# Entering a seven-product up projection by halves of the tokens, with four pairs' first products computed ahead

## The chip, the core and the metric

The kernel runs on one core of a Trainium2 chip as a single launch. The metric is the device time of that core in microseconds (us), and less is better. The engines and their names in the profile: TensorE (PE, and PEld for its weight loads), VectorE (DVE), ScalarE (ACT), GpSimd (POOL) and SyncE (SP), which issues the DMAs; "SPq" is its queue.

## The reference

The program is one layer of a first block (a retention and pooling mixer, cross attention, a convolutional gated feed-forward network) followed by two layers of a second block. The change is at the seam of cross attention and the feed-forward network. Cut to what matters there:

```python
x = x + cross_attn(...)                 # its last step is o @ wo
h = rmsnorm(x, ffn_norm_g)              # x * rsqrt(mean(x*x) + eps) * g
a = h @ w_up                            # 1024 tokens x 1024 features -> 2 x 22 x 128
c = conv_w[0]*a2 + conv_w[1]*a1 + conv_w[2]*a + conv_b   # a1, a2: a shifted by 1, 2 tokens
gate, val = jnp.split(c, 2, axis=-1)
x = x + (jax.nn.silu(gate) * val) @ w_down
```

## The kernel before

Activations stand transposed: `xT[0..7]` are eight tiles of 128 features by 1024 tokens. Every fp32 operand is split into a high part (a cast on ACT) and a low part (a subtraction on DVE), and a product is three matmuls per 128 features: high by high, low by high, high by low. One product of a 128x512 result over 512 features is 12 matmuls.

**The projection `xa_wo`** (L793-798) makes x after cross attention, in eight blocks `ft` of 128 output features by two halves of 512 tokens. For each block and half, `residual_add` (L653) adds the result to `xT`, squares it on ACT and sums the squares into `acc` on POOL, and the half is stored to DRAM. Blocks 0 to 5 run both halves in turn, blocks 6 and 7 run the first half of both and then the second.

**The norm** (`norm_half`, L882) then takes one token half at a time: four transposes of `acc` on PE (L889), a sum on DVE (L890), a reciprocal square root by ten small DVE instructions (L304-309), a broadcast by four small matmuls (L894), a copy to `rb` (L895), and eight multiplications of `xT` by `rb` and the gain (L897).

**The up projection** takes its 44 output blocks as 22 pairs of a gate and a value block and computes a pair with seven products instead of eight. The normalised input is seen as a 2x2 block matrix: B11 and B21 are features 0-511 and 512-1023 of the first token half, B12 and B22 the same of the second. The products use B11, B21, B22 and four sums of them, T1 to T4 (`token_blocks`, L903). T1, T3, B22 and T4 share storage with `ahi_t`/`alo_t`, the input of the projection before. Products 1 and 2 read only B11 and B21; the other five read T1 to T4 or B22. Of the weights, four units per pair are split into `whi`/`wlo` (three buffers each): unit 0 is the raw gate weights (products 1 and 2), unit 1 `sm` (products 5 and 6), unit 2 product 7, unit 3 products 3 and 4. The sums of weights are made on POOL (L838-840, L866). Products accumulate in PSUM; ACT copies the running sum out after a product ("P1", "U2", "W", L939-941), and DVE adds such a copy to another product to get a result half (L952, L975, L984). Each result goes through the convolution (ACT L929, DVE L930 and L931), the gate through silu (L967), the two are multiplied (L977) and stored to `hid_d` (L978).

**The down projection** (L1032) reads `hid_d` back (`hidden`, L1009), splits it, and accumulates over groups of 6, 8 and 8 hidden blocks; `x` is re-loaded from DRAM for its residuals (L1033, L655).

What sets the order: up to the second block a scheduler orders every engine's instructions by its own cost estimates, and each engine then runs its list in order. Only from the second block on (L1101) is PE held to written order.

The result of one half in one step, and a product:

```python
mm(ps, whi[:, k], hi[:, k], ...)   # L878
mm(ps, whi[:, k], lo[:, k], ...)   # L879
mm(ps, wlo[:, k], hi[:, k], ...)   # L880
```

## Time and profile before

| what | value |
|---|---|
| time, median of 3 runs | 2691.21 us (2689.56 to 2697.92) |
| the profiled execution | 2690.13 us, of which the span is 2688.3 us |
| PE busy | 2577.1 us, 96% of the span |
| DVE, ACT, POOL busy | 1747.6, 1113.5, 518.0 us |

The three runs differ by 8 us; the profiled execution lies 1.1 us under their median. Times inside the trace count from the start of the span. "PEclk" is the granted TensorE clock as a share of full speed. A bracket such as [5.21 <-DVE hr L309] says that the engine was idle for 5.21 us before this instruction, and what released it.

### The profile page before, as it was taken

What the parts mean: (1) busy time and instruction counts of PE and PEld (TensorE: products, weight loads), DVE (VectorE), ACT (ScalarE), POOL (GpSimd) and SP (SyncE); (2) the same over time, 40 slices, a digit from 0 to 9 for tenths busy, and PEclk for the clock granted to TensorE, in tenths of its full rate; (3) what the DMA queues carried; (4) which work ended last, traced back from release to release, by engine and by line L of the source; (5) the groups of instructions that cost most, each with busy time, mean ns of one, the idle gap of its engine ahead of it and who ended that gap; (6) DMA issues with size and microseconds to landing.
All of it is one profiled execution on the core that took longest, in us unless ns stands there. A gap on an engine that the chain in (4) does not pass through costs nothing. (4 is left out here: it accounts for less than half of the span.)

```text
span 2688.3 us, 36856 instructions
## 1 busy us (share of the span) xinstructions
PE 2577.1 (96%) x13750; PEld 2162.3 (80%) x13750; DVE 1747.6 (65%) x3501; ACT 1113.5 (41%) x2279; POOL 518.0 (19%) x426
## 2 busy tenths in 40 slices
PE   7999999998699999999999999999988999999998
PEld 7888888886588878778778888878876788888898
DVE  8544735434677777842458798575776887777755
ACT  6221334432454444521227774344545443434432
POOL 4112021013333434100121010000143211121101
PEclk9999999998799999999999999999998999999999
DMA  7211141221122222451224443776533222221331
GB/s 252 95 40 37 58 145 44 60 85 55 39 71 88 77 75 90 167 201 47 79 72 126 118 137 105 213 251 199 171 109 114 93 77 81 87 82 64 106 114 71
DMA packets 174118, 282.17 MB, mean 105 GB/s; under 512 B 35522, under 2 KB 103652, under 8 KB 173684
## 3 DMA queue, kind: packets, MB, share of 16 engines
q1 hardware_dynamic: 173940, 279.82, 32.0%
q8 instruction: 108, 1.77, 0.3%
q14 instruction: 70, 0.57, 0.1%
HBM read 206.78 MB, written 72.99 MB: 104 GB/s over the span
## 5 line engine op out<-in xcount | busy, mean ns | idle before, releaser
L1090 PE MATMUL g<-ahi_t,whi 128*128 128x512 f32 x1120 | 466.6, 417 | 3.7 <-DVE y L1624 3.7
L1092 PE MATMUL g<-ahi_t,wlo 128*128 128x512 f32 x1120 | 443.2, 396 | 0.0
L1091 PE MATMUL g<-alo_t,whi 128*128 128x512 f32 x1120 | 441.3, 394 | 0.0
L239 ACT CAST whi<-wraw 128x1024 fp32r<-128x1024 f32 (+1 forms) x172 | 178.6, 1038 | 516.3 <-PE g L272 389.8
L272 PE MATMUL g<-alo_t,whi 128*128 128x512 f32 x832 | 324.1, 391 | 0.6 <-DVE alo_t L293 0.6
L271 PE MATMUL g<-ahi_t,whi 128*128 128x512 f32 x832 | 323.6, 391 | 0.0
L240 DVE TENSOR_TENSOR wlo<-wraw,whi 128x1024 fp32r<-128x1024 f32 (+1 forms) x172 | 212.5, 1237 | 106.1 <-ACT whi L239 105.2
L275 PE MATMUL g<-ahi_t,wlo 128*128 128x512 f32 x832 | 263.1, 390 | 0.0
L1092 PEld LDWEIGHTS g<-ahi_t,wlo 128*128 128x128 f32 x1120 | 212.5, 190 | 47.7
L1090 PEld LDWEIGHTS g<-ahi_t,whi 128*128 128x128 f32 x1120 | 213.4, 190 | 43.7 <-issue 4.4
L1091 PEld LDWEIGHTS g<-alo_t,whi 128*128 128x128 f32 x1120 | 213.5, 191 | 36.7
L655 DVE TENSOR_TENSOR xT<-g,xT 128x512 f32<-128x512 f32 x80 | 51.9, 687 | 234.9 <-PE g L275 218.8
L271 PEld LDWEIGHTS g<-ahi_t,whi 128*128 128x128 f32 x832 | 156.2, 188 | 32.7 <-DVE xT L655 0.5
L272 PEld LDWEIGHTS g<-alo_t,whi 128*128 128x128 f32 x832 | 156.1, 188 | 32.5 <-DVE alo_t L293 0.9
L275 PEld LDWEIGHTS g<-ahi_t,wlo 128*128 128x128 f32 x832 | 156.0, 188 | 32.2
L930 DVE SCALAR_TENSOR_TENSOR c<-a,par,c 128x1024 f32<-128x1024 f32 x44 | 84.8, 1926 | 102.4 <-ACT c L929 102.4
L642 POOL TENSOR_TENSOR acc<-acc,sq 128x512 f32<-128x512 f32 x42 | 73.2, 1762 | 372.9 <-ACT sq L640 372.9
L238 POOL TENSOR_TENSOR wraw<-wraw,par 128x1024 f32<-128x1024 f32 x32 | 65.5, 2048 | 220.1 <-DMA wraw<-in_w_blocks_dram 69.7
L292 ACT CAST pth<-m 128x512 fp32r<-128x512 f32 (+2 forms) x112 | 48.4, 433 | 98.6 <-PE m L1886 81.1
L838 POOL TENSOR_TENSOR sm<-rv 128x512 f32<-128x512 f32 x22 | 29.5, 1342 | 282.8 <-DMA rv<-in_w_blocks_dram 282.8
L271 PE MATMUL g<-hh,whi 128*128 128x512 f32 x192 | 75.0, 401 | 8.4 <-DVE xT L655 8.4
L878 PE MATMUL m<-ahi_t,whi 128*128 128x512 f32 x176 | 69.5, 396 | 8.7 <-ACT ahi_t L292 8.5
(594 smaller groups left out, 6072.7 us busy)
## 6 DMA issues: line engine op xcount, KB each, us to landing
wraw<-in_w_blocks_dram SPq DMA_DIRECT2D x164, 512.0 KB
rv<-in_w_blocks_dram SPq DMA_DIRECT2D x22, 512.0 KB
rg<-in_w_blocks_dram SPq DMA_DIRECT2D x22, 512.0 KB
hid_d<-c SPq DMA_DIRECT2D x22, 512.0 KB
hraw<-hid_d SPq DMA_DIRECT2D x22, 512.0 KB
x_d<-xT SPq DMA_DIRECT2D x32, 256.0 KB
kq_d<-kq SPq DMA_DIRECT2D x16, 512.0 KB
kq<-kq_d SPq DMA_DIRECT2D x16, 512.0 KB
```

Of the source, the lines that this page charges most:

```text
L238: nc.gpsimd.tensor_tensor(raw, raw, prm(gain, 0, nk).unsqueeze(2).to_broadcast(list(raw.shape)), op=ALU.mult)
L239: nc.scalar.copy(hi, raw)
L240: nc.vector.tensor_sub(lo, raw, hi.bitcast(F32))
L271: mm(ps[hf], whi[:, kt, :], hi[kt][:, c], start=(kt == order[0]), stop=False)
L272: mm(ps[hf], whi[:, kt, :], lo[kt][:, c], start=False, stop=False)
L275: mm(ps[hf], wlo[:, kt, :], hi[kt][:, c], start=False, stop=(kt == order[-1]))
L642: nc.gpsimd.tensor_tensor(acc[:, c], acc[:, c], sq, op=ALU.add)
L878: mm(ps, whi[:, k], hi[:, k], start=(start and k == 0), stop=False, **more)
L930: v.scalar_tensor_tensor(out=c, in0=a[:, 1:1 + S], scalar=par[:, 1, 44 + j:45 + j], in1=c, op0=ALU.mult, op1=ALU.add)
L1090: mm(po, whi[:, i, cs], ahi[kt][:, c], start=(i == 0), stop=False)
L1091: mm(po, whi[:, i, cs], alo[kt][:, c], start=False, stop=False)
L1092: mm(po, wlo[:, i, cs], ahi[kt][:, c], start=False, stop=(i == len(kts) - 1))
```

## The change

The norm's work is cut into `norm_stat`, a generator whose first step makes the transposes and the reciprocal square root and whose second makes the broadcast. PE is held to written order from the projection `xa_wo` on. There, blocks 0 to 3 run both halves in turn; then blocks 4 to 7 run the first half, the first token half's transposes stand, and blocks 4 to 7 run the second half (their weights are loaded and split twice). The broadcast for the first half stands two blocks later, still inside the projection.

For the first half the multiplications and the splits of B11 and B21 are made as before. For the second half, ACT multiplies features 0-511 by the gain and DVE forms B22 minus B12 from values that are not yet normalised (L924, L925). Then products 1 and 2 of the first four pairs (`AHEAD`) are computed, copied and added into a buffer `two` of 128x2x512 and stored to a DRAM array `up_d` (L935). `two` is a name with a single buffer, which holds in turn the broadcast of the first half, the four pairs' results, and `both`, into which products 1 of pairs 0 and 1 are loaded back. The second half's transposes stand behind pair 0's products, its broadcast behind pair 1's. After that the second half is normalised and T2, T3, T1, B22 and T4 are formed by other sums of the same blocks: T3 from the difference made earlier, T2 by one addition, T4 on POOL as before (L955).

Pairs 0 and 1 then go through their five remaining products side by side, pairs 2 and 3 one at a time; a re-loaded result is added by DVE where an ACT copy stood. Pairs 4 to 21 keep all seven products in the order 1, 2, 6, 3 of the pair before, 5, 4 of the pair before, 7. There are four buffers `a` for conv inputs instead of three, and the load-ahead of down weights is by three and stands at the end of the pairs instead of by two behind the first six hidden blocks. Core of the diff:

```diff
+AHEAD = 4
-        for ft in range(6):
+        mano.enter_context(tc.manual_schedule(engines={mybir.EngineType.PE}))
+        for ft in range(4):
             gemm_ft(lambda hf, ps: xo_put(ft, hf, ps))
-        w67 = [wtake(), wtake(1)]
-        for hf in range(2):
-            for ft in (6, 7):
-                half_ft(w67[ft - 6], hf, lambda hf, ps: xo_put(ft, hf, ps))
+        for ft in range(4, 8):
+            half_ft(wtake(), 0, lambda hf, ps: xo_put(ft, hf, ps))
+        stat = norm_stat(acc, 0)
+        for ft in range(4, 8):
+            half_ft(wtake(), 1, lambda hf, ps: xo_put(ft, hf, ps))
+            if ft < 6:
+                rps = next(stat)
...
+    def two():
+        return stp.tile([128, 2, 512], F32, tag="two", name="two")
...
-    norm_half(0)
+    rb = two()[:, 0]
+    nc.scalar.copy(rb, rps)
+    for k in range(8):
+        v.scalar_tensor_tensor(out=xT[k][:, h0], in0=xT[k][:, h0], scalar=prm("ffn_norm_g", k), in1=rb, op0=ALU.mult, op1=ALU.mult)
+        put("B11" if k < 4 else "B21", k % 4, xT[k][:, h0])
+    for k in range(4):
+        nc.scalar.activation(out=xT[k][:, h1], in_=xT[k][:, h1], func=AF.Copy, scale=prm("ffn_norm_g", k))
+        v.scalar_tensor_tensor(out=xT[k][:, h1], in0=xT[k + 4][:, h1], scalar=prm("ffn_norm_g", k + 4), in1=xT[k][:, h1],
+                               op0=ALU.mult, op1=ALU.subtract)
     up_make(3)
-    norm_half(1)
-    token_blocks()
+    stat = norm_stat(acc, 1)
+    for j in range(AHEAD):
+        X, y, st = pg(), pg(), two()
+        product(X, 1, j, True)
+        nc.scalar.copy(st[:, 0], X)
+        product(y, 2, j, True)
+        v.tensor_tensor(st[:, 1], y, st[:, 0], op=ALU.add)
+        nc.sync.dma_start(out=up_d[j], in_=st)
+        up_make()
+        if j < 2:
+            rps = next(stat)
+    rb = acc[:, h0]
+    nc.scalar.copy(rb, rps)
+    for k in range(4):
+        v.tensor_tensor(xT[k][:, h1], xT[k][:, h1], rb, op=ALU.mult)
+        v.tensor_tensor(xT[k][:, h0], xT[k][:, h1], xT[k][:, h0], op=ALU.add)
+        put("T2", k, xT[k][:, h0])
+    for k in range(4):
+        put("T3", k, xT[k][:, h1])
+    for k in range(4):
+        b22 = xT[k + 4][:, h1]
+        v.scalar_tensor_tensor(out=b22, in0=b22, scalar=prm("ffn_norm_g", k + 4), in1=rb, op0=ALU.mult, op1=ALU.mult)
+        t1 = res.tile([128, 512], F32, tag="sq", name="t1", bufs=2)
+        v.tensor_tensor(t1, b22, xT[k][:, h0], op=ALU.subtract)
+        put("T1", k, t1)
+    for k in range(4):
+        put("B22", k, xT[k + 4][:, h1])
+        nc.gpsimd.tensor_tensor(xT[k + 4][:, h0], xT[k + 4][:, h0], xT[k][:, h0], op=ALU.subtract)
+    for k in range(4):
+        put("T4", k, xT[k + 4][:, h0])
...
+    both = two()
+    for j in range(2):
+        nc.sync.dma_start(out=both[:, j], in_=up_d[j, :, 0])
+    for j in range(2):
+        p6(j, both[:, j])
+    for j in range(2):
+        p7(j)
+        up_make()
+    for j in range(2):
+        p5(j)
+        c22(j)
+        up_make()
+    for j in range(2):
+        p3(j)
+    for j in range(2):
+        p4_(j)
+        up_make()
+    for j in range(2, NFF + 1):
+        if AHEAD <= j < NFF:
+            p12(j)
+            up_make()
...
+    wahead(wnext[0] + 3)
-    wahead(wnext[0] + 2)
```

How the instructions stand on PE before, from the last matmuls of `xa_wo` on: behind them come the transposes (L889), the broadcast (L894) and the first pair's products.

```order
L284 MATMUL g<-ahi_t,whi 128x512
L285 MATMUL g<-alo_t,whi 128x512
L286 MATMUL g<-ahi_t,wlo 128x512
L889 MATMUL m<-cst,acc 128x128 x4
L894 MATMUL m<-cst,hr 128x128 x4
L889 MATMUL m<-cst,acc 128x128 x4
L878 MATMUL g<-B11h,whi 128x512
L878 MATMUL g<-B21h,whi 128x512
L879 MATMUL g<-B11l,whi 128x512
L880 MATMUL g<-B11h,wlo 128x512
```

And now, on PE, the transposes of the first token half, behind the last of the first-half matmuls; the `g` matmuls below them are second halves of the projection.

```order
L288 MATMUL g<-ahi_t,whi 128x512
L289 MATMUL g<-alo_t,whi 128x512
L290 MATMUL g<-ahi_t,wlo 128x512
L664 MATMUL m<-cst,acc 128x128 x4
L288 MATMUL g<-ahi_t,whi 128x512
L289 MATMUL g<-alo_t,whi 128x512
L290 MATMUL g<-ahi_t,wlo 128x512
```

And the transposes of the second token half, between the products 2 of pair 0 and 1 of pair 1.

```order
L910 MATMUL g<-B21h,whi 128x512
L911 MATMUL g<-B21l,whi 128x512
L912 MATMUL g<-B21h,wlo 128x512
L664 MATMUL m<-cst,acc 128x128 x4
L910 MATMUL g<-B11h,whi 128x512
L911 MATMUL g<-B11l,whi 128x512
```

The small matmuls of the norm have moved from the end of the projection into it, and between products that read only the first token half.

On ACT before, the last casts for T1 to T4 and the copies of the first sums out of PSUM (`xT4` to `xT7` into `ahi_t` are T4, `xT2` and `xT3` into it T1 and into `T2h` T2, `t3` is T3):

```order
L292 CAST ahi_t_81<-t3_5120 128x512
L292 CAST ahi_t_81<-xT5_2709 128x512
L292 CAST ahi_t_81<-t3_5135 128x512
L292 CAST ahi_t_81<-xT2_2706 128x512
L292 CAST ahi_t_81<-xT3_2707 128x512
L292 CAST T2h_4980<-xT2_2706 128x512
L292 CAST whi_5246<-rg_5034 128x512
L292 CAST whi_5246<-rv_5035 128x512
L292 CAST T2h_4980<-xT3_2707 128x512
L292 CAST ahi_t_81<-xT6_2710 128x512
L292 CAST ahi_t_81<-xT7_2711 128x512
L941 COPY P1_5167<-g_5154 128x512
```

On ACT now, the same place (`xT4` to `xT7` into `ahi_t` are T4, `t1` is T1, `two_5237` is the buffer of pair 3's stored results):

```order
L296 CAST ahi_t_81<-xT4_2709 128x512
L296 CAST T2h_5033<-xT2_2707 128x512
L296 CAST ahi_t_81<-xT5_2710 128x512
L296 CAST T2h_5033<-xT3_2708 128x512
L296 CAST whi_5265<-rrv_5178 128x512
L296 CAST ahi_t_81<-xT6_2711 128x512
L296 CAST ahi_t_81<-xT7_2712 128x512
L932 COPY two_5237<-g_5235 128x512
L296 CAST ahi_t_81<-t1_5295 128x512
L296 CAST ahi_t_81<-t1_5300 128x512
L296 CAST ahi_t_81<-t1_5305 128x512
L296 CAST ahi_t_81<-t1_5310 128x512
```

Pair 3's copy now stands behind all four T4 casts and ahead of the T1 casts, and a cast of T2 behind the first of T4.

On DVE before, the end of the sums (the last two `alo_t` rows are T4, `a` is a conv input):

```order
L293 TENSOR_TENSOR T2l_4981<-xT2_2706,T2h_4980 128x512
L293 TENSOR_TENSOR wlo_5247<-rg_5034,whi_5246 128x512
L293 TENSOR_TENSOR wlo_5247<-rv_5035,whi_5246 128x512
L293 TENSOR_TENSOR T2l_4981<-xT3_2707,T2h_4980 128x512
L293 TENSOR_TENSOR alo_t_82<-xT6_2710,ahi_t_81 128x512
L293 TENSOR_TENSOR alo_t_82<-xT7_2711,ahi_t_81 128x512
L952 TENSOR_TENSOR a_5182<-g_5169,P1_5167 128x512
L952 TENSOR_TENSOR a_5280<-g_5267,P1_5265 128x512
L293 TENSOR_TENSOR wlo_5284<-rv_5186,whi_5283 128x512
L984 TENSOR_TENSOR a_5243<-m_5230,W_5228 128x512
```

On DVE now, from the last T4 low part on (`two_5237` as above, `two_5338` is `both`, `wlo_5383` is product 7's weights of pair 1):

```order
L297 TENSOR_TENSOR alo_t_82<-xT7_2712,ahi_t_81 128x512
L934 TENSOR_TENSOR two_5237<-g_5236,two_5237 128x512
L297 TENSOR_TENSOR alo_t_82<-t1_5295,ahi_t_81 128x512
L297 TENSOR_TENSOR alo_t_82<-t1_5300,ahi_t_81 128x512
L951 TENSOR_TENSOR t1_5305<-xT6_2711,xT2_2707 128x512
L951 TENSOR_TENSOR t1_5310<-xT7_2712,xT3_2708 128x512
L297 TENSOR_TENSOR alo_t_82<-t1_5305,ahi_t_81 128x512
L297 TENSOR_TENSOR alo_t_82<-t1_5310,ahi_t_81 128x512
L1017 TENSOR_TENSOR two_5338<-g_5341,two_5338 128x512
L297 TENSOR_TENSOR wlo_5383<-rrv_5226,whi_5382 128x512
L1017 TENSOR_TENSOR two_5338<-g_5355,two_5338 128x512
```

The two additions to `both`, and the weight split behind the first of them, stand behind pair 3's addition and the T1 low parts.

## Rows read from the trace of the kernel before

**Rows 1.** The page, part 1: busy time and share of each engine over the whole span.

```profile
PE 2577.1 (96%) x13750; PEld 2162.3 (80%) x13750; DVE 1747.6 (65%) x3501; ACT 1113.5 (41%) x2279; POOL 518.0 (19%) x426
```

**Rows 2.** Windows: entry, the 22 pairs, start of the down projection.

```profile
core 0: us, PE busy (x) PEld busy (x) DVE busy (x) ACT busy (x) POOL busy (x), PEclk, DMA share, GB/s
648.00:714.00 66.00, 34.91 (x111) 24.71 (x110) 49.06 (x88) 23.75 (x39) 22.82 (x14) 0.66 0.06 20
714.00:1122.00 408.00, 406.29 (x1765) 330.41 (x1764) 299.11 (x275) 201.01 (x257) 143.41 (x118) 1.00 0.24 83
1134.00:1160.00 26.00, 17.64 (x69) 13.88 (x69) 14.71 (x17) 8.96 (x10) 0.00 (x0) 0.87 0.96 353
```

**Rows 3.** Timeline of TensorE, 639 to 715: start, duration, work, [idle before <-releaser].

```profile
639.80 0.39 PE L284 MATMUL g<-ahi_t,whi 128*128 128x512 f32 x1
...
648.42 0.39 PE L286 MATMUL g<-ahi_t,wlo 128*128 128x512 f32 x1
648.65 0.60 PE L889 MATMUL m<-cst,acc 128*128 128x128 f32 x4
654.46 2.04 PE L894 MATMUL m<-cst,hr 128*128 128x128 f32 x8 [5.21 <-DVE hr L309]
...
706.65 0.80 PE L878 MATMUL g<-T2h,whi 128*128 128x512 f32 x1 [7.08 <-ACT P L941]
...
710.65 0.51 PE L878 MATMUL g<-T2h,whi 128*128 128x512 f32 x1
...
714.27 0.39 PE L878 MATMUL g<-ahi_t,whi 128*128 128x512 f32 x1
```

**Rows 4.** Timeline of VectorE, the same stretch.

```profile
654.15 0.16 DVE L309 SCALAR_TENSOR_TENSOR hr<-rs_a,hr 128x4 f32<-128x4 f32 x1
657.16 5.39 DVE L897 SCALAR_TENSOR_TENSOR xT<-xT,par,rb 128x512 f32<-128x512 f32 x8 [2.85 <-ACT rb L895]
...
663.07 2.49 DVE L293 TENSOR_TENSOR B11l<-xT,B11h 128x512 fp32r<-128x512 f32 x4
```

**Rows 5.** Timeline of GpSimd, the same stretch.

```profile
650.61 1.71 POOL L642 TENSOR_TENSOR acc<-acc,sq 128x512 f32<-128x512 f32 x1
...
688.25 6.49 POOL L912 TENSOR_TENSOR xT<-xT,xT 128x512 f32<-128x512 f32 x2 [12.36 <-DVE xT L911]
...
706.74 1.28 POOL L838 TENSOR_TENSOR sm<-rv 128x512 f32<-128x512 f32 x1 [1.18 <-DMA rv<-in_w_blocks_dram]
```

**Rows 6.** Timeline of SyncE's queue (SPq): a weight load.

```profile
702.54 0.33 SPq L835 DMA_DIRECT2D rv<-in_w_blocks_dram  x1
```

**Rows 7.** SyncE's queue in a later stage: store of x, next load into its buffer.

```profile
1732.18 1.83 SPq L1571 DMA_DIRECT2D x_d<-x  x2
...
1735.64 0.92 SPq L1569 DMA_DIRECT2D x<-x_d  x2
```

**Rows 8.** VectorE, the instruction that takes this load.

```profile
1739.85 0.75 DVE L1570 SCALAR_TENSOR_TENSOR x<-x,par,rfb 128x512 f32<-128x512 f32 x1 [3.45 <-DMA x<-x_d]
```

**Rows 9.** Groups of instructions by line, 714 to 1122: count, busy us, mean ns, idle before.

```profile
L930 DVE SCALAR_TENSOR_TENSOR c<-a,par,c 128x1024 f32<-128x1024 f32 x42 | 82.2, 1957 | 102.4 <-ACT c L929 102.4
...
L840 POOL TENSOR_TENSOR sm<-rv 128x512 f32<-128x512 f32 x19 | 39.2, 2065 | 1.5
...
L293 DVE TENSOR_TENSOR wlo<-sm,whi 128x1024 fp32r<-128x1024 f32 x20 | 25.3, 1265 | 0.0
...
L941 ACT COPY U<-g 128x512 f32<-128x512 f32 x21 | 12.3, 587 | 87.9 <-PE g L880 87.9
```

**Rows 10.** Waits of TensorE, 540 to 1160 us: total, times, longest.

```profile
PE g L271 <- DVE xT L655: 8.4, 1, 8.4
...
PE g L878 <- ACT W L941: 0.9, 1, 0.9
```

**Rows 11.** VectorE ahead of the down projection's first residuals.

```profile
1145.85 1.23 DVE L293 TENSOR_TENSOR alo_t<-hraw,ahi_t 128x1024 fp32r<-128x1024 f32 x1 [1.11 <-ACT ahi_t L292]
1146.99 2.48 DVE L655 TENSOR_TENSOR xT<-g,xT 128x512 f32<-128x512 f32 x4
```

More of the change, by code (lines that the diff above doesn't have):

```diff
@@ L98, in _blocks @@
             full(name, ft * 128)
+    for ft in range(4, 8):
+        full("xa_wo", ft * 128)
     for i in range(NFF):
@@ L651, in row_bcast, with norm_stat @@
             nc.scalar.copy(dst[:, a * 512:(a + 1) * 512], ps.rearrange("p a b -> p (a b)"))
+    def norm_stat(acc, hf):
+        ss = tiny.tile([128, 4], F32, tag="hss", name="hss", bufs=2)
+        r = tiny.tile([128, 4], F32, tag="hr", name="hr", bufs=2)
+        ps = pm((128, 4, 128))
+        for j in range(4):
+            nc.tensor.transpose(ps[:, j], acc[:, hf * 512 + j * 128:hf * 512 + (j + 1) * 128], ident)
+        nc.vector.tensor_reduce(out=ss, in_=ps, axis=AX.X, op=ALU.add)
+        rsqrt(r, ss, 1.0 / D, EPS)
+        yield
+        ps = pm((128, 4, 128))
+        for j in range(4):
+            mm(ps[:, j], r[:, j:j + 1].to_broadcast([128, 128]), ident, start=True, stop=True)
+        yield ps.rearrange("p a b -> p (a b)")
     def residual_add(ft, hf, ps, acc, sq=None):
@@ L917, in tile_block, with put @@
-    norm_half(0)
-    up_make(3)
-    norm_half(1)
-    token_blocks()
+    def put(nm, k, x):
+        split(op[nm][0][:, k], op[nm][1][:, k], x)
+    rb = two()[:, 0]
[7 more added lines that the diff above has]
+                               op0=ALU.mult, op1=ALU.subtract)
@@ L988, in tile_block, with p6 @@
-    for j in range(NFF + 1):
-        if j < NFF:
-            up_first(j)
-            up_make(1)
-        up_pair(j)
+        v.tensor_tensor(u["ag"][:, 2:514], y, P1, op=ALU.add)
+    def p6(j, U2=None):
+        if j >= AHEAD:
+            u = ups[j]
+            product(u["X"], 6, j, False)
+            u["U2"] = keep("U2", 2, u["X"])
+            return
+        u = ups[j] = {}
+        if U2 is None:
+            U2 = p4.tile([128, 512], F32, tag="U2", name="U2", bufs=2)
+            nc.sync.dma_start(out=U2, in_=up_d[j, :, 0])
+        ps = pg()
+        product(ps, 6, j, True)
+        u["U2"] = U2
+        v.tensor_tensor(U2, ps, U2, op=ALU.add)
@@ new lines, in p5, with p7, c22, p3 @@
+    def p5(j):
+        u = ups[j]
+        if j < AHEAD:
+            u["X"] = pg()
+        product(u["X"], 5, j, j < AHEAD)
+        u["W"] = keep("W", 2, u["X"], u["U2"] if j < AHEAD else None)
+    def p7(j):
+        u = ups[j]
+        u["Y"] = pm()
+        product(u["Y"], 7, j, True)
+    def c22(j):
+        u = ups[j]
+        u["av"] = new_a()
+        v.tensor_tensor(u["av"][:, 514:], u["Y"], u["W"], op=ALU.add)
+    def p3(j):
+        u = ups[j]
+        product(u["X"], 3, j, False)
+        if j < AHEAD:
+            u["ag"] = new_a()
+            nc.sync.dma_start(out=u["ag"][:, 2:514], in_=up_d[j, :, 1])
+            v.tensor_tensor(u["ag"][:, 514:], u["X"], u["U2"], op=ALU.add)
+        else:
+            nc.scalar.copy(u["ag"][:, 514:], u["X"])
+        gates(j)
@@ new lines, in p4_ @@
+    def p4_(j):
+        u = ups[j]
+        product(u["Y"], 4, j, False)
+        v.tensor_tensor(u["av"][:, 2:514], u["Y"], u["U2"], op=ALU.add)
+        values(j)
+    both = two()
[15 more added lines that the diff above has]
+        up_make()
```

139 lines of the change are left out of this document (51 added, 88 removed).

## The prediction

> **What bounds the kernel now.** Over the whole span PE is busy for 96% of the time [rows 1], so I looked for where the other 4% are, in the table of windows. In the 408 us of the 22 pairs PE is busy for 406.3 us at a granted clock of 1.00, and DVE for 299.1 us; in the 66 us before them PE is busy for 34.9 us, at a mean clock of 0.66 (between its levels of 1.2 and 2.4 GHz), and no engine is full [rows 2]. So the pairs are bound by PE and their entry by a chain. The timeline of PE shows that chain: the last matmul of the projection starts at 648.42, and only at 714.27 do the matmuls run on without a stop. In between PE waits 5.21 us for the reciprocal square root and, last, 7.08 us behind the sums of token blocks [rows 3]. The number of instructions in the window gives the useful part: 111, less 24 small ones and the last three or four of the projection, and one just behind its end: 84 matmuls. At full clock they follow each other at (648.42 - 639.80) / 38 = 0.227 us [rows 3], so they need 19.1 us. The stretch from 648.65 to 714.27 takes 65.6 us. **The entry loses 65.6 - 19.1 = 46.5 us**, and this is all that the change can give: the pairs themselves wait for next to nothing (0.9 us for a copy of W is their longest [rows 10]).
>
> **The change part by part.** The count of product matmuls and of projection matmuls stays; only their places change. The sum is made on the profiled execution, 2690.1 us (span 2688.3 and 1.8 around it), 1.1 us under the median of the runs. E is the end of the last matmul of the projection.
>
> *First half.* Its transposes, square root and broadcast stand inside the projection. From the last transpose of before to the end of the square root it was 654.31 - 648.65 = 5.7 us [rows 3, 4]; two blocks by one half are 2 x 24 x 0.227 = 10.9 us, so they hide it. What DVE must do before pair 0 is eight multiplications and the low parts: 5.4 us and at least 2.5 us for the four of B11 [rows 4], 7.9 us, beside the last two blocks of 10.9 us. I take about 1 us lost there (0 to 3) and 1 us for the small matmuls that remain.
>
> *Pair 0, then a wait.* Its 24 matmuls end at E + 5.5. Then PE's written order holds the second half's transposes, and these need `acc` complete. Before, the last block's addition, square and sum were done at 652.32, 3.7 us behind E [rows 3, 5]. Now that addition stands on DVE behind B21's low parts, two weight splits and a difference of the second half, some 6.5 us at the durations of rows 4 and 9; with the square and the sum (1.7 us) `acc` is complete at about E + 9. PE waits some 3.6 us. Behind the transposes stand pair 1's products (5.4 us), which hide the square root; broadcast and copy (0.6 us, as the U copy in rows 9) end at about E + 16.8.
>
> *The sums.* From then on DVE has to make, before it may add product 6 of pair 0 to `both`: 16 multiplications and sums, 20 low parts, the additions of pairs 2 and 3, one 512-wide and one 1024-wide weight split. That is 39 x 0.6 (a 512-wide one, 2.49 / 4 [rows 4]) plus 1.3 [rows 9], with the four three-operand ones at 0.67: about 24.9 us, to E + 41.7 if nothing waits. PE has work for pairs 2 and 3 until E + 25 or so and then stands: T2's last low part is in this run, and product 7 of pair 1 needs a weight split that stands behind the addition to `both`, as the order shows.
>
> *The way over DRAM.* `both` may be loaded only when pair 3's store has landed, since `two` has one buffer. A store of x and the next load into its buffer are 1735.64 - 1733.1 = 2.5 us apart (the second of two stores starts 0.92 us after 1732.18), and the load is used 4.2 us after its issue [rows 7, 8]; the weight load at 702.54 was used at 706.74, again 4.2 us [rows 5, 6]. So 6.7 us from pair 3's addition to the sum with `both`. Seven instructions of DVE (4.2 us) lie beside it; the rest, about 2.5 to 3.3 us, is a new wait. Without any other, the sum with `both` starts at E + 45.
>
> *T4 on GpSimd.* Pair 3's copy stands on ACT behind four T4 casts, and each of these needs a subtraction on POOL. Alone a subtraction of this size takes 1.28 us; two of them took 6.49 us while DVE ran its own two-operand instructions beside them [rows 5]. Lower bound: they finish beside DVE's other work, 0 us. Upper: four at 3.25 us, 13 us, less what hides of the first: 12 us. I take 10, near the upper end, as DVE runs just such instructions here. The Trainium skill ("SBUF — State Buffer", "Who interferes with whom") says that DVE and GpSimd share a port pair under an exclusive lock; by that rule the subtractions wait for gaps on DVE, which the 6.49 us agree with, and the sum would be the upper one. The skill's "DMA: Bandwidth & Descriptors" ("Anatomy of one DMA — SWDGE (gpsimd) path") fits 2.0 us plus bytes / 436e3, so an estimate of 3.2 us for the store of 512 KB and 2.6 us for a load of 256 KB; by it the round trip is 5.8 us and the sum 0.9 us less. Its figure is for another path than SyncE's, and the trace's 4.2 us decide for the load.
>
> *Sum of the entry.* The sum with `both` at E + 45 to E + 57, the weight split behind it, and 12 matmuls of product 7 (2.7 us): product 7 of pair 1 ends at E + 49 to E + 61. PE's own work up to there is 144 matmuls, 32.7 us. So the new entry loses 16 to 28 us there and 2 us about E: 18 to 30 us. With T4 at 10 us it is 28 us.
>
> *The clock behind a wait.* From 706.65, behind 7.08 us of waiting, nine matmuls took 4.0 us until 710.65 instead of 9 x 0.227 = 2.0 [rows 3]: the lower level of the clock, 1.2 GHz. The new waits will have such a stretch too, partly inside times that DVE sets: 1.5 us (0 to 4).
>
> *Pairs 0 to 3.* They have 60 matmuls left each, 13.6 us, and DVE's work of a pair is 299.1 / 21 = 14.2 us [rows 2]. For pairs 0 and 1 there are 72 matmuls (16.3 us) behind product 7, beside the convolutions of both. With four buffers `a` I take 2.5 us lost (0 to 5).
>
> *Pairs 4 to 21.* PE's order has 12 matmuls (2.7 us) between a product and the one that accumulates on it; the copy between takes 0.59 us [rows 9]. No change.
>
> *The down projection.* PE waits 8.4 us there now for the first residual on DVE [rows 10], which stands behind splits of hidden blocks, each 1.23 us behind 1.1 us of waiting, so 2.3 us apart, at a DMA share of 0.96 [rows 2, 11]. One more weight load goes ahead of the x loads, and one more such split stands in front: 2 us lost (0 to 4).
>
> *The sum.* Lost anew: 28 + 1.5 + 2.5 + 2 = 34 us, against 46.5 before. **Gain 12.5 us: 2690.1 - 12.5 = 2677.6 us.**
>
> **The rivals.**
>
> *B, the chain is light.* POOL gets in between DVE's instructions, as it does in the pairs, where such a one takes 2.07 us beside DVE [rows 9]. The entry then loses 18 to 20 us, DVE's backlog none: 46.5 - 20 - 1 = 25.5 us gained, 2664.6. For it: DVE itself waits for the T4 casts, and in such a gap POOL is alone (1.28 us). Against it: the 6.49 us in the same kind of stretch [rows 5].
>
> *C, no change that can be told.* The chain loses 28 us and DVE's backlog is not absorbed: pairs 0 and 1 need 2 x 14.2 = 28.4 us of DVE beside 16.3 us of PE, 12 us late. 46.5 - 28 - 1.5 - 12 - 2 = 3 us gained: 2687. For it: these pairs add two re-loaded results on DVE that ACT copied before. Against it: part of that work belongs behind the next products and has four buffers to wait in.
>
> *D, slower: the written order costs in every pair.* PE now takes what the program says, no longer what the scheduler chose. Should the copies of U or P be late behind other work of ACT, PE stands in each of 18 pairs. A wait of 2 us per pair costs 36 us, 2678 + 36 = 2714. It decides from (12.5 + 8.1) / 18 = 1.1 us per pair. Against it: 0.59 us of copy against 2.7 us of cover, and ACT was idle 87.9 us in all before the U copies, waiting for PE [rows 9].
>
> **How the numbers follow.** What the runs here can tell from no change is 0.3%, 8.1 us, so faster means under 2683. The forecast (entry loses about 28 us) has 0.48, its own range 2669 to 2683; B 0.26; C 0.18; D 0.08. Faster is the forecast and B, 0.74; the same is C, 0.18; slower D, 0.08. The range reaches from B's lower end (46.5 - 18 = 28.5 gained with no other loss, 2661.6; 2660 with a little to spare) to beyond C, 2690, and leaves out D and the tails.
>
> **What would show it.** In the profile after: no idle PE time between the last projection block and pair 0 over 3 us; a wait of 3 to 4 us before the second half's transposes; then the longest wait of PE, 15 to 27 us in one or two pieces, at T2's low part or at product 7 of pair 1, released by DVE; POOL's T4 subtractions over 2 us each; about 4.2 us from the load of `both` to the DVE addition; the windows of pairs 4 to 21 with PE at 99%; and a wait of 8 to 12 us at the down projection. The forecast is wrong if the waits before p7 of pair 1 are under 10 us (B), if DVE is full through pairs 0 to 3 while PE waits there (C), or if PE waits in each pair from 4 on (D).

## The result and the profile after

The changed kernel takes 2676.16 us, the median of five runs (2670.62 to 2678.85), beside 2693.95 us for five runs of the kernel before on the same chips. The ratio is 0.9931 [0.9912, 0.9949]: faster by 0.7%, more than the 0.3% that can be told from no change. The profiled execution took 2678.85 us with a span of 2677.1, 11.2 us under that of before.

The busy times of the whole span, as in [rows 1], of the kernel after:

```profile
PE 2569.2 (96%) x13750; PEld 2158.4 (81%) x13750; DVE 1745.2 (65%) x3517; ACT 1113.9 (42%) x2275; POOL 484.4 (18%) x426
```

PE has as many instructions as before, and is busy for 7.9 us less. The gain can't be read here; the windows show it. Of the kernel after, the entry and the steady pairs, in the columns of [rows 2]:

```profile
648.00:714.00 66.00, 48.71 (x196) 38.25 (x195) 58.74 (x80) 25.60 (x42) 26.32 (x17) 0.87 0.28 95
757.00:1085.00 328.00, 328.00 (x1430) 268.16 (x1429) 220.42 (x226) 160.10 (x204) 91.58 (x103) 1.00 0.23 83
```

And the steady pairs of the kernel before:

```profile
757.00:1085.00 328.00, 327.17 (x1421) 265.96 (x1420) 245.86 (x220) 159.30 (x204) 127.61 (x102) 1.00 0.23 79
```

In the same 66 us of the entry PE does 196 matmuls instead of 111, at a mean granted clock of 0.87 instead of 0.66, so more of them ran at the higher of the clock's levels, 2.4 GHz. In the pairs it is busy throughout, nearly as it was, and does 1430 matmuls instead of 1421 in the same 328 us. The longest waits of PE from 540 to 1160 us, as in [rows 10], of the kernel after (total, times, longest):

```profile
PE g L911 <- DVE T2l L297: 11.7, 1, 11.7
PE g L275 <- DVE xT L675: 7.6, 1, 7.6
PE g L276 <- DVE hl L297: 4.1, 2, 2.5
PE m L670 <- DVE hr L313: 2.3, 2, 1.8
PE m L664 <- POOL acc L647: 2.2, 1, 2.2
```

The first is the entry's, the second and third are the down projection's, the last two the norm's (1.8 and 2.2 us of them the second half's, 0.5 the first half's). Where the entry's waits lie is shown by the timeline of TensorE, kernel after (start, duration, work, [idle before <-releaser]):

```profile
652.62 0.40 PE L910 MATMUL g<-B11h,whi 128*128 128x512 f32 x1
...
660.63 0.66 PE L664 MATMUL m<-cst,acc 128*128 128x128 f32 x4 [2.25 <-POOL acc L647]
...
694.50 0.80 PE L911 MATMUL g<-T2l,whi 128*128 128x512 f32 x1 [11.74 <-DVE T2l L297]
...
707.50 0.50 PE L912 MATMUL m<-ahi_t,wlo 128*128 128x512 f32 x1 [0.98 <-DVE wlo L297]
...
709.93 0.39 PE L910 MATMUL g<-ahi_t,whi 128*128 128x512 f32 x1
```

Pair 0 starts at E = 652.62 us without a wait. Product 7 of pair 1 ends at 709.93, E + 57.3. That is 144 matmuls, 32.6 us at 0.2267 each, so 24.7 us are lost. Where the 11.2 us between the two profiled executions come from, by stretches of the traces:

| stretch | before to after |
|---|---|
| code ahead of the last projection, the same in both | +1.8 us |
| last projection | +2.1 us |
| E to the last product of the pairs | 474.5 to 450.9 us, -23.5 |
| down projection | 253.65 to 260.5 us, +6.9 |
| the rest | +1.5 us |

The first row and the last are code that the change doesn't touch. Between the medians the gain is 17.8 us; single executions of one kernel lie up to 13 us apart (2685.57 to 2698.26 us in one session of the kernel before). The experiments are therefore compared by stretches counted from their own E, each from one trace, beside the ratio: p7(1) is the end of product 7 of pair 1 after E, and "336 done" the end of the 336th product matmul after E, four pairs' worth (before: 123.4, after: 103.9). Between kernels that have the same entry, p7(1) differs by up to 0.6 us and "336 done" by up to 1.6, so smaller differences than these show nothing.

Of the 23.5 us, 19.5 lie in the first 336 product matmuls and 4.0 behind them (351.1 to 347.0 us; 0.7 of this is three matmuls of the down projection that stood among the products before). There each 84 matmuls take 19.29 us in the kernel after. Before, eleven of the eighteen stretches of 84 took as long, and the others up to 20.0 us, the last, with those three, 21.1: beside the wait of 0.9 us in [rows 10], PE waited there in the kernel before for

```profile
PE g L880 <- DVE wlo L293: 0.4, 1, 0.4
PE m L878 <- DVE a L984: 0.3, 1, 0.3
```

All the kernels below take 347.0 us for this part too, the one without products ahead included. So these 4 us come from what they share with the changed kernel, and not from the products ahead.

### The profile page after: what moved, and what is told of

Same layout as the page of the kernel before. It is cut to its first block, busy times and chain, and to the rows that moved or that the text cites. A ratio compares the mean times of both kernels' runs of the same rounds, so it can differ in the third digit from the quotient of the medians.

```text
span 2677.1 us, 36876 instructions
## 1 busy us (share of the span) xinstructions
PE 2569.2 (96%) x13750; PEld 2158.4 (81%) x13750; DVE 1745.2 (65%) x3517; ACT 1113.9 (42%) x2275; POOL 484.4 (18%) x426
## 5 line engine op out<-in xcount | busy, mean ns | idle before, releaser
L1185 PE MATMUL g<-ahi_t,whi 128*128 128x512 f32 x1120 | 465.8, 416 | 3.7 <-DVE y L1716 3.7
L1187 PE MATMUL g<-ahi_t,wlo 128*128 128x512 f32 x1120 | 442.5, 395 | 0.0
L1186 PE MATMUL g<-alo_t,whi 128*128 128x512 f32 x1120 | 440.4, 393 | 0.0
L276 PE MATMUL g<-alo_t,whi 128*128 128x512 f32 x800 | 312.2, 391 | 2.6 <-DVE alo_t L297 2.6
L275 PE MATMUL g<-ahi_t,whi 128*128 128x512 f32 x800 | 311.6, 391 | 0.0
L244 DVE TENSOR_TENSOR wlo<-wraw,whi 128x1024 fp32r<-128x1024 f32 (+1 forms) x176 | 220.2, 1252 | 105.0 <-ACT whi L243 104.0
L279 PE MATMUL g<-ahi_t,wlo 128*128 128x512 f32 x800 | 252.3, 390 | 0.0
L1187 PEld LDWEIGHTS g<-ahi_t,wlo 128*128 128x128 f32 x1120 | 212.0, 189 | 47.6
L1185 PEld LDWEIGHTS g<-ahi_t,whi 128*128 128x128 f32 x1120 | 212.8, 190 | 43.4 <-issue 4.4
L1186 PEld LDWEIGHTS g<-alo_t,whi 128*128 128x128 f32 x1120 | 213.0, 190 | 36.5
L276 PEld LDWEIGHTS g<-alo_t,whi 128*128 128x128 f32 x800 | 150.2, 188 | 33.6 <-DVE alo_t L297 3.4
L275 PEld LDWEIGHTS g<-ahi_t,whi 128*128 128x128 f32 x800 | 150.3, 188 | 31.1 <-ACT ahi_t L296 0.2
L279 PEld LDWEIGHTS g<-ahi_t,wlo 128*128 128x128 f32 x800 | 150.0, 188 | 30.9
L966 DVE SCALAR_TENSOR_TENSOR c<-a,par,c 128x1024 f32<-128x1024 f32 x44 | 60.0, 1363 | 105.4 <-ACT c L965 105.4
L276 PE MATMUL g<-hl,whi 128*128 128x512 f32 x192 | 76.6, 399 | 4.1 <-DVE hl L297 4.1
L297 DVE TENSOR_TENSOR ptl<-m,pth 128x512 fp32r<-128x512 f32 (+2 forms) x112 | 55.5, 495 | 31.9 <-ACT pth L296 31.3
```

Source lines behind the costliest of these rows:

```text
L244: nc.vector.tensor_sub(lo, raw, hi.bitcast(F32))
L275: mm(ps[hf], whi[:, kt, :], hi[kt][:, c], start=(kt == order[0]), stop=False)
L276: mm(ps[hf], whi[:, kt, :], lo[kt][:, c], start=False, stop=False)
L279: mm(ps[hf], wlo[:, kt, :], hi[kt][:, c], start=False, stop=(kt == order[-1]))
L297: return a, nc.vector.tensor_sub(lo, src, hi.bitcast(F32))
L966: v.scalar_tensor_tensor(out=c, in0=a[:, 1:1 + S], scalar=par[:, 1, 44 + j:45 + j], in1=c, op0=ALU.mult, op1=ALU.add)
```

## The experiments

Two theories stood at first. A: the gain is the four pairs' products that fill the wait for the second half's sums, less what DVE's chain of sums delays. S: the gain is the norm inside the projection and PE's written order, and the products ahead add little.

**No products ahead** (all seven products of each pair in order, from pair 0 on), and **two pairs ahead:**

```diff
-AHEAD = 4
+AHEAD = 0        (e1; both broadcasts ahead of pair 0)
+AHEAD = 2        (e12)
```

> Nothing is computed ahead: the norm stands inside the projection and the sums are formed the new way, PE keeps written order, but both token halves' small matmuls precede pair 0 and all pairs run all seven products in order. Theory A (the products computed ahead cover the sums on VectorE, and this is what the change gains): PE has only pair 0's products 1 and 2 (5.4 us) to do before it needs T2, and the second half's square root is exposed; T2 complete about 33 us behind the end of the projection, so the entry loses about 30 us before product 6, some 8 to 10 us more than the changed kernel: 2683 to 2688 us. Rival S (the gain comes from the norm inside the projection and the written order, and the products ahead give nothing): within 3 us of the changed kernel, 2673 to 2679 us.

> Two pairs ahead instead of four, all else as in the changed kernel. Theory A (each product ahead is worth its time on PE as long as PE would wait for T2): 48 matmuls (10.9 us) less lie before T2, VectorE and ScalarE have two additions and two copies less to make (about 1.5 us), so the wait for T2's low part is 20 to 22 us instead of 11.7, and pairs 2 and 3 with all seven products lose about 2 us less to VectorE: 7 to 9 us more than the changed kernel, 2682 to 2686 us. Rival (pairs 2 and 3 ahead give nothing, because VectorE sets the end of the first four pairs anyway): within 2 us of the changed kernel.

Measured: 2695.0 us with none, ratio to before 1.0005 [0.9995, 1.0015], 336 done at E + 122.1; 2686.72 us with two pairs, 0.9974 [0.9963, 0.9985], 336 done at E + 113.2. PE's waits with none ahead:

```profile
PE g L908 <- ACT P L978: 22.3, 1, 22.3
PE m L664 <- POOL acc L647: 11.7, 1, 11.7
```

S is refuted: without the products ahead the rest of the change gains nothing as a whole. By the stretches it gains 1.3 us up to 336 done and the 4.0 us behind it, and loses 6.6 us in the down projection (253.65 to 260.3). With two pairs ahead PE is 113.2 - 103.9 = 9.3 us later than with four, a little over the 7 to 9 expected, and two pairs' products 1 and 2 are 48 x 0.227 = 10.9 us of PE. The kernel without products ahead came out slower than A said, and the trace gives a reason for at least 5 us of it. ACT, kernel without products ahead:

```profile
699.06 1.22 ACT L296 CAST ahi_t<-t 128x512 fp32r<-128x512 f32 x2 [3.57 <-DVE t L951]
700.19 0.58 ACT L978 COPY P<-g 128x512 f32<-128x512 f32 x1
```

The copy of pair 0's product 1, which PE needs for the next one, stands on ACT behind casts that wait for DVE's T1; it ends at 700.77. T2's last low part was done at 694.27 + 1.75 = 696.0, 4.8 us earlier:

```profile
694.27 1.75 DVE L297 TENSOR_TENSOR T2l<-xT,T2h 128x512 fp32r<-128x512 f32 x1
```

So this kernel also has a late copy that the changed one has not, and the value of the products ahead is better read from the step from two to four. How the 4.0 us in the later pairs divide between the written order and the other edits of the pairs, no run told apart.

**The sums' order on DVE.** Is the wait DVE's chain as a whole, or only that T2's last low part stands late in it? DVE is held to: the four multiplications, the four T2 sums, then T2's low parts, and the rest.

```diff
+    hand = tc.manual_schedule(engines={mybir.EngineType.DVE})
...
+    for k in range(4):
         v.tensor_tensor(xT[k][:, h0], xT[k][:, h1], xT[k][:, h0], op=ALU.add)
+    for k in range(4):
         put("T2", k, xT[k][:, h0])
```

> VectorE is held to an order in which the four T2 sums and their low parts stand ahead of T3, B22, T1 and T4; nothing else changes. Theory A (VectorE's order of the sums sets when product 6 can start): the 11.7 us wait for T2's low part shrinks to 0 to 3 us, and a wait of 5 to 9 us appears at product 7 of pair 1, whose weights' low part stands behind the T4 low parts; product 7 of pair 1 ends 4 to 6 us earlier than in the changed kernel (709.9), the total 2670 to 2673 us. Rival R (the way of the first results over DRAM sets the entry): the wait only moves to product 7 of pair 1, whose end moves by under 2 us, and the total stays within 2 us.

Measured: 2672.0 us, 0.9920 [0.9905, 0.9934]; p7(1) at E + 52.25 and 336 done at E + 100.0, so 5.1 and 3.9 us earlier, as expected. PE's waits with T2 first:

```profile
PE m L912 <- DVE wlo L297: 3.7, 2, 2.2
PE g L911 <- DVE T2l L297: 3.4, 3, 1.4
```

The wait for T2's low parts falls from 11.7 us to 3.4 in three pieces. Waiting for weight splits takes part of its place: 3.7 us at product 7, where 5 to 9 were expected, and 3.1 at other products, instead of 2.4 in all. The order is part of the wait, the rest is the chain's length.

**DVE beside GpSimd.** In the kernel after the chain itself is longer than forecast. DVE, kernel after:

```profile
671.05 6.30 DVE L942 TENSOR_TENSOR xT<-xT,acc 128x512 f32<-128x512 f32 x4 [0.78 <-ACT acc L940]
677.27 2.73 DVE L949 SCALAR_TENSOR_TENSOR xT<-xT,par,acc 128x512 f32<-128x512 f32 x4
...
706.15 0.69 DVE L1017 TENSOR_TENSOR two<-g,two 128x512 f32<-128x512 f32 x1 [2.50 <-DMA two<-up_d]
```

And GpSimd at that time, kernel after (L866 to L899 are weight sums, L955 is T4):

```profile
670.42 1.27 POOL L865 TENSOR_TENSOR sm<-rrv 128x512 f32<-128x512 f32 x1 [3.12 <-DVE wlo L297]
671.77 1.62 POOL L866 TENSOR_TENSOR rrv<-rwraw,rrv 128x512 f32<-128x512 f32 x1
673.47 1.62 POOL L867 TENSOR_TENSOR sm<-rrv 128x512 f32<-128x512 f32 x1
675.17 1.62 POOL L899 TENSOR_TENSOR rwraw<-rwraw,sm 128x512 f32<-128x512 f32 x1
...
680.68 10.81 POOL L955 TENSOR_TENSOR xT<-xT,xT 128x512 f32<-128x512 f32 x4 [3.88 <-DVE xT L943]
```

The four multiplications take 1.58 us each where they stand beside POOL's weight sums; the four L949 behind them, with POOL idle, take 0.68. T4's subtractions take 2.70 us each. In the kernel without products ahead POOL is idle beside the four multiplications (from 672.19 us), and they take 2.50 us together, 0.63 each, with the same operands. To tell contention from the chain, one kernel reads the broadcast in PSUM, where it is made, and another puts T4 on DVE:

```diff
-    rb = acc[:, h0]              (e3)
-    nc.scalar.copy(rb, rps)
+    rb = rps
...
-        nc.gpsimd.tensor_tensor(xT[k + 4][:, h0], xT[k + 4][:, h0], xT[k][:, h0], op=ALU.subtract)   (e6)
+        v.tensor_tensor(xT[k + 4][:, h0], xT[k + 4][:, h0], xT[k][:, h0], op=ALU.subtract)
```

> The multiplications of the second half read the broadcast straight from PSUM instead of from a copy in SBUF. Theory A with the lock (the four multiplications take 1.56 us each instead of 0.6 because GpSimd makes weight sums beside them and both need the second SBUF port): with one operand in PSUM they take 0.6 to 0.7 us each beside the same GpSimd work, the copy (0.6 us and its hop) goes, T2's low part is ready 4 to 5 us earlier, total 3 to 5 us less. Rival (they are slow for another reason): they stay at 1.5 us each, and only about 1 us goes with the copy.

> The four T4 subtractions are made on VectorE instead of GpSimd. Theory A with the lock: VectorE does 4 x 0.6 = 2.4 us more, but its own instructions beside them are no longer stretched (3.6 us in the changed kernel) and the T4 casts on ScalarE, ahead of which T2's casts wait, come earlier: T2's low part 1 to 4 us earlier, total 1 to 4 us less. Rival (GpSimd's work is off the chain): VectorE's extra 2.4 us show in full, total 2 to 3 us more.

Measured: broadcast in PSUM 2674.35 us, 0.9931 [0.9913, 0.9948], p7(1) at E + 53.4 (3.9 us earlier); T4 on DVE 2670.06 us, 0.9918 [0.9904, 0.9931], p7(1) at E + 53.5 (3.8 earlier). By the stretch both did about what their theory said; in the ratio a gain of 0.15% can't be told. DVE and GpSimd in the kernel that reads the broadcast in PSUM:

```profile
670.43 1.88 DVE L941 TENSOR_TENSOR xT<-xT,m 128x512 f32<-128x512 f32 x3
672.23 2.71 DVE L948 SCALAR_TENSOR_TENSOR xT<-xT,par,m 128x512 f32<-128x512 f32 x4
674.86 1.78 DVE L942 TENSOR_TENSOR xT<-xT 128x512 f32<-128x512 f32 x1
```

```profile
670.66 1.29 POOL L865 TENSOR_TENSOR sm<-rrv 128x512 f32<-128x512 f32 x1 [4.48 <-DVE wlo L297]
672.03 1.31 POOL L866 TENSOR_TENSOR rrv<-rwraw,rrv 128x512 f32<-128x512 f32 x1
```

The same multiplication takes 0.63 us instead of 1.58 beside the same POOL work, and POOL 1.31 instead of 1.62; the next sum with both operands in SBUF (L942) takes 1.78 again. Not all of the 3.9 us is contention: this kernel has no copy to wait for either, and its multiplications start at E + 17.0 instead of 18.4. T4 on DVE adds four instructions, 2.4 us, and the whole list with them is still 1.2 us shorter (31.4 us instead of 32.6), since nothing runs beside it on POOL then. The rest of its 3.8 us is two of T1's low parts, 1.3 us, that stand behind the sum with `both` there, and 1.2 us less of waiting for the load.

**The way over DRAM.** Is the 2.50 us wait of DVE for `two` of the kernel after on the path? The load of the kernel after, in the columns of [rows 6]:

```profile
702.58 0.79 SPq L1055 DMA_DIRECT2D two<-up_d  x2
```

Now products 1 of pairs 0 and 1 go into tiles of their own instead of one more turn of `two`:

```diff
-        p6(j, both[:, j])
+        p6(j)          # re-loads into its own U2, three buffers
```

> Product 1 of pairs 0 and 1 is loaded back into tiles of its own (three buffers) instead of into the single buffer that pair 3's store still holds. Theory A (VectorE's sums set the entry, the way over DRAM adds only the 2.5 us for which VectorE waits for the load): the wait for T2 stays at 11 to 12 us, the 2.5 us of VectorE at the first addition go, product 7 of pair 1 ends 1.5 to 2.5 us earlier. Rival R (the way over DRAM sets the entry): product 7 of pair 1 ends 5 us or more earlier.

Measured: 2672.02 us, 0.9921 [0.9906, 0.9936]; p7(1) at E + 55.56, 1.75 us earlier, as expected: about two thirds of the 2.50 us were on the path.

**All three together,** and the same with T4 on DVE:

> The three edits that each shortened the entry stand together: T2 first on VectorE, the broadcast read from PSUM, tiles of their own for the re-loaded results. Theory A (VectorE's sums are one chain, on which the savings of order and of contention add, while the way over DRAM falls out of the chain once T2 comes first): product 7 of pair 1 ends 47 to 49 us behind the projection instead of 57.3, the total is 8 to 10 us below the changed kernel, 2665 to 2669 us. Rival (the savings are the same microseconds, taken three times): it ends at 51 to 52 us as with T2 first alone, total 2670 to 2673 us.

> The three edits of the run before, and T4 on VectorE too. Theory A: with T2 first T4 is no longer ahead of T2, so what is left of T4's gain is the unstretched work on VectorE less the 2.4 us added: within 2 us of the three edits alone. Rival (GpSimd's T4 sets the end of the entry still, by the casts that stand ahead of pair 1's weight split): 2 to 5 us less.

Measured: 2664.78 us, ratio to before 0.9903 [0.9889, 0.9916], p7(1) at E + 50.6 and 336 done at E + 96.6; with T4 on DVE 2669.21 us, 0.9908 [0.9894, 0.9921], E + 50.9 and 97.6, the same by the stretch. The first is 1.0% faster than the kernel before; it is 7.3 us ahead of the changed kernel at 336 done, and the two ratios differ by 0.28%, with intervals that overlap a little. The parts alone add to 5.1 + 3.9 + 1.75 = 10.7 us, together they bring 6.7, between the two expectations. PE's waits in the first, of the entry:

```profile
PE g L912 <- DVE wlo L297: 6.5, 3, 5.0
...
PE g L911 <- DVE T2l L297: 2.7, 3, 1.3
```

A new wait has come up, 5.0 us for the low part of the weights of pair 1's product 6: that split now stands on DVE behind T2, T3's low parts and B22's multiplications. One more kernel held DVE to a longer order by hand (T2, T3, T1, B22, T4 with the stored pairs' additions and weight splits between), to bring product 7 forward. It has the broadcast in PSUM and own tiles too, and leaves PE's order in the down projection to the scheduler:

> All that the runs pointed to: the broadcast read from PSUM, own tiles for re-loaded results, VectorE held to T2, then T3, then B22, T1 and T4, with pairs 2 and 3's additions and the weight splits of products 6 and 7 placed between, and PE's order in the down projection left to the scheduler. Theory A (the order of the sums is what is left of the entry): product 7 of pair 1 ends 39 to 45 us behind the projection instead of 57.3 (50.6 with the three edits); pairs 0 to 3 then lose more, since VectorE has the same work in less time, so that their end comes 11 to 14 us earlier than in the changed kernel; with the down projection 14 to 20 us less, 2656 to 2662 us. Rival (VectorE's whole work up to pair 3 sets the end of pair 3, whatever the order): the end of pair 3 comes where the three edits had it (96.6 us behind the projection), and only the down projection's 4 to 6 us are gained over them: about 2660 us.

Measured: 2674.02 us, 0.9939 [0.9926, 0.9951]. p7(1) came to E + 44.25, within the 39 to 45 us of theory A, but 336 were done only at E + 106.6, later than in the changed kernel, so both expectations missed the time. Behind product 7 PE waited for T1's high part (2.1 us, until E + 46.6). The additions of pairs 0 and 1 stood last on DVE, and product 3, which goes into the PSUM tile that W is read from, waited for them (5.2 us for W). Here the longer order only moved the wait.

**The down projection.** It lost 6.2 us more than before, counted by its 1056 matmuls, three of which stood among the products before (21.1 us against 14.9 over 0.2267 us each), where 2 were forecast. The expectations below have 20.0, 13.6 and, for the weights as before, 19.5; the traces, with 1056 matmuls in each, give 21.1, 14.9 and 20.2. Theory B: the weight load that was moved ahead of the pairs' end. Rival: PE's written order, and DVE's list at that point. One kernel loads the weights as before, one ends the written order at the down projection, one does so in the kernel with all three parts:

```diff
-    wahead(wnext[0] + 3)          (e8)
+    wahead(wnext[0] + 2)          behind the first six hidden blocks
...
+    mano.close()                  (e9, e11) ahead of the down projection
```

> Only the load-ahead of down weights is put back as it was: by two, behind the first six hidden blocks. In the changed kernel the down projection, from its first to its last matmul, takes 260.3 us against 256.9 before, and PE's lost time in it is about 21 us against 15. Theory B (the third weight load and its split, ahead of the x loads, cost this): the stage takes 255 to 258 us. Rival (the stage starts closer behind the last pair's results, and waits for the same hidden blocks and x whatever the weights do): 259 to 262 us.

> The changed kernel, with PE given back to the scheduler's order for the down projection alone (from the last pair to the second block); the scheduler may again put matmuls with high parts ahead of those that need low parts not yet split. In the changed kernel the down projection's PE work loses 20.0 us against matmuls at 0.227 us apart, before 13.6, and putting the weight loads back gave 19.5. Theory B2 (written order makes PE take each hidden block's low part at once, so it waits for the splits of blocks that arrive late): the loss goes back to 13 to 16 us, the total 4 to 6 us below the changed kernel. Rival (the pairs now end nearer to their last results, and the hidden blocks are late for any order): the loss stays at 19 to 21 us, the total within 2 us.

> The three edits to the entry (T2 first, broadcast from PSUM, own tiles) together with PE's order in the down projection left to the scheduler. Theory: the two places are independent, so their savings add: the entry as with the three edits (product 7 of pair 1 about 50.6 us behind the projection), the down projection losing 17 to 18 us instead of 19.9: 2 to 3 us below the three edits, 2661 to 2664 us. Rival (the time the pairs give back is waited out at the down projection's first residuals, whose loads from DRAM set it): no gain over the three edits, 2664 to 2667 us.

Measured: weights as before 2676.75 us, 0.9945 [0.9931, 0.9958], loss 20.2 of 21.1, the stage 259.6 us, above the 255 to 258 of B: B falls. The kernels that leave this stage alone take 260.0 to 261.7 us for it. Scheduler's order 2676.02 us, 0.9937 [0.9922, 0.9953], loss 17.7. TensorE at the start of the down projection and at the start of its third group of hidden blocks, kernel after:

```profile
1110.67 0.51 PE L276 MATMUL g<-hl,whi 128*128 128x512 f32 x1 [2.53 <-DVE hl L297]
...
1115.33 0.50 PE L276 MATMUL g<-hl,whi 128*128 128x512 f32 x1 [1.61 <-DVE hl L297]
...
1132.75 0.79 PE L275 MATMUL g<-hh,whi 128*128 128x512 f32 x1 [7.60 <-DVE xT L675]
...
1273.92 0.50 PE L276 MATMUL g<-alo_t,whi 128*128 128x512 f32 x1 [1.41 <-DVE alo_t L297]
...
1276.79 0.50 PE L276 MATMUL g<-alo_t,whi 128*128 128x512 f32 x1 [1.21 <-DVE alo_t L297]
```

The same places with the scheduler's order:

```profile
1101.88 1.09 PE L275 MATMUL g<-hh,whi 128*128 128x512 f32 x4
1102.80 0.63 PE L276 MATMUL g<-hl,whi 128*128 128x512 f32 x2
...
1129.33 0.79 PE L275 MATMUL g<-hh,whi 128*128 128x512 f32 x1 [10.49 <-DVE xT L675]
...
1270.77 0.73 PE L276 MATMUL g<-alo_t,whi 128*128 128x512 f32 x2 [0.63 <-DVE alo_t L297]
```

The scheduler takes four high-by-high matmuls first, so that a late low part finds work ahead of it; in written order PE stands at each. The first two waits go (4.1 us), but 2.9 us of them come back at the residual, whose time DVE sets; at the third group 2.62 us of waits become 0.63. What is left, 3.4 us (260.5 to 257.1), is the written order's part, about as much as the later pairs gained. With all three parts the ratio can't tell it, 2664.72 us, 0.9894 [0.9879, 0.9909] beside 0.9903 [0.9889, 0.9916]; by the stretch the down projection is 2.0 us shorter (260.0 to 258.0), in the theory's 2 to 3, while 336 were done at E + 98.2 instead of 96.6 with the same entry. The other 3 us are open: DVE comes to this place with a full list in both kernels, and no run told apart why the residual stands later in it.

## Why the prediction came out right, step by step

The time (2676.16 against 2677.6) and the likeliest case were right, and so was the mechanism in the main: the products ahead fill the wait for DVE's chain of sums, and that chain, not PE, sets the new entry. That the sum came out so near is partly luck. Of the sizes, the entry and the pairs gained more than forecast and the down projection lost more; between the two profiled executions this made 11.2 us, where 12.5 were forecast. Between the medians the gain is 17.8 us: the execution of before from which the sum starts, 2690.1 us, lies 3.8 us under the median of all five. And within the entry a chain that was taken too short stood against a T4 that was taken too dear.

- *Norm inside the projection:* right. No wait between the last projection block and pair 0; the projection stage is 2.1 us longer, 2 were forecast. The wait ahead of the second transposes is 2.25 us (3.6 forecast). That pair 1's products would hide the second half's square root was wrong: three of its small instructions on DVE stood behind GpSimd's weight sums (lines in the last section), and PE waited 1.79 us for it.
- *The sums:* too short. DVE runs from 671.05 without a stop for 32.6 us; 24.9 were forecast at 0.6 us an instruction. Contention was charged to T4 alone; it also stretched the multiplications beside GpSimd's weight sums, 6.30 us for four instead of 2.5, so 3.8 us. Beside T4 four instructions of DVE (two low parts, a split and a sum) took 6.85 us instead of 3.2, so 3.7 us. With both, 24.9 become 32.4.
- *The way over DRAM:* right. 2.5 to 3.3 us of new wait forecast, 2.50 measured; load to use 706.15 - 702.58 = 3.6 us where 4.2 were taken from [rows 7, 8].
- *T4:* right in kind. Four subtractions took 10.81 us, near the upper end of 13. On the path it was far less than the 10 us taken, and by another way: the sum with `both` waited for DVE's list and the load, not for pair 3's copy behind the T4 casts, and T4 cost that list 3.7 us. The kernel with T4 on DVE agrees: 2.4 us of its own and a list 1.2 us shorter make 3.6.
- *The sum with `both`:* at E + 53.5 (45 to 57 forecast, 55 taken), p7(1) at E + 57.3 (about 59 by the same sum). The chain's length and T4's share erred in opposite directions, which is luck.
- *Entry:* 2.1 + 24.7 = 26.8 us lost, 28 + 1.5 forecast. PE's longest wait is one piece of 11.7 us at T2's low part, not 15 to 27: the order on DVE lets product 6 start before the sum with `both`, and the rest of the loss lies in the norm's waits and small matmuls, in late weight splits, and in the lower level of the clock behind two of the waits. From 694.50, behind 11.74 us, and from 670.05, behind 1.79 us, 12 and 6 matmuls stood 0.43 us apart at a granted clock of 0.50, 1.2 GHz; this cost 2.5 + 1.2 = 3.7 us, where 1.5 were taken. Behind the entry's other waits most stood 0.23 us apart.
- *Pairs 0 to 3:* 3.1 us lost, 2.5 forecast.
- *Pairs 4 to 21:* no change was forecast, and 3.4 us were gained: 84 matmuls take 19.29 us throughout, 0.25 over 84 x 0.2267, and the small waits that these pairs had before are gone.
- *Down projection:* the term that was mis-sized most for its range, 2 us (0 to 4) forecast, 6.2 measured, and its reason fell. The prediction named the weight load and one more split; putting them back gave 0.9 us, no more than such stretches differ by. It did not see that the written order, weighed for each pair as rival D, runs on into the next stage, where low parts do come late (3.4 us); the other 3 us are open.
- *What it left out:* before, the pairs from 714.27 on lost 8.9 us over 0.2267 us a matmul (three down-projection matmuls, 0.7 us, among them), which the sum booked as nothing; after, the same term is 7.3 us (450.9 - 24.7 - 1848 x 0.2267). So the pairs gave 1.6 us where 2.5 were to be lost: 3.1 lost in pairs 0 to 3, where 0.7 were lost in as many matmuls before, and the gain of pairs 4 to 21.

Of the rivals, B (light chain) needed 18 to 20 us lost in the entry; 24.7 to 26.8 lie between it and the forecast, and the kernel with all three parts loses as little as B said, 18 us (50.6 - 32.6), but by its edits. C (backlog not absorbed) did not show, and neither did D (a stall in each pair): the pairs lost their small waits instead.

## What to carry to other kernels

Work that needs only the part of the input that is ready fills a chain's wait for about its own length (9.3 of 10.9 us here), at the price of what it adds to the engine that forms the chain. Shorten that chain by what its consumer takes first, and count each instruction on it at its price beside the engines that run then, not at its price alone. An order written out for one stage should end with it, or be checked where the next stage's operands arrive late: here the later pairs went 3.4 us faster in the changed kernel, and the down projection lost 3.4 us by the order.

## What the runs showed of the hardware

A DVE instruction with two operands in SBUF slows beside GpSimd's two-operand instructions, and slows them: 0.6 us to 1.58, and 1.28 to 1.62. With one operand in PSUM neither does (0.63 and 1.31). The Trainium skill ("SBUF — State Buffer", "Who interferes with whom") states that the two engines share a port pair under a lock; by its rule an instruction of DVE with at most one SBUF input, outside DVE's two-port modes, doesn't contend, and the trace agrees, 0.63 beside 1.58 us. The Trainium skill ("SBUF — State Buffer", "Summary: rules for kernel authors") also states that the second to come waits until the first has finished; two streams one behind the other would then need 0.6 + 1.28 = 1.88 us a pair, and POOL's follow each other at (673.47 - 671.77) = 1.70 us, so here a part of each runs beside the other.

Where single short DVE instructions came second here, they waited for nearly the whole of GpSimd's. In the square root of the second half, kernel after:

```profile
664.63 1.30 POOL L867 TENSOR_TENSOR sm<-rrv 128x512 f32<-128x512 f32 x1
664.82 1.14 DVE L311 TENSOR_TENSOR rs_a<-hr 128x4 f32<-128x4 f32 x1
...
667.36 0.16 DVE L311 TENSOR_TENSOR rs_a<-hr 128x4 f32<-128x4 f32 x1
```

The same 128x4 multiplication takes 1.14 us beside GpSimd's sum and 0.16 in a later round of the square root, with GpSimd idle. The long one ends about 0.02 us behind GpSimd's. Two more instructions of this square root do the same behind the sums before and after it (1.09 and 1.14 us; the first of them, L308, reads one tensor only). The three cost it some 2.9 us, and PE waited 1.79 us for its end.

The same effect can vanish by phase. Conv additions on DVE and weight sums on GpSimd, 757 to 1085 us, kernel after (columns as [rows 9]):

```profile
L966 DVE SCALAR_TENSOR_TENSOR c<-a,par,c 128x1024 f32<-128x1024 f32 x35 | 45.5, 1300 | 98.0 <-ACT c L965 98.0
L867 POOL TENSOR_TENSOR sm<-rrv 128x512 f32<-128x512 f32 x17 | 21.9, 1289 | 1.3
```

Before they took 2054 and 2105 ns in this stretch (1957 and 2065 over all pairs [rows 9]). The instructions have the same shapes, but they have moved apart in time: before, the two convolution additions of a block ran beside a GpSimd instruction for 79.0 of their 121.5 us, now for 0.9 of 90.4. The kernel without products ahead has no such overlap at all, so it is not these products that moved them; which other edit did, no run told apart. DVE's busy time falls from 245.9 to 220.4 us. PE was the bound of these pairs and gained little: 9 matmuls more in 328 us, about 2 us. That contention caused the small waits that went is not shown.
